# Loading the first pair of heads of the last pass in two halves, in a softmax-matmul kernel on one Trainium2 core

## The chip, the core and the metric

The kernel runs on one core of one Trainium2 chip. The core has five engines with instruction streams of their own: TensorE (PE, and PEld for its weight loads), VectorE (DVE), ScalarE (ACT), GpSimd (POOL) and SyncE (SP). They wait for each other through semaphores. Transfers between HBM and the on-chip memory are issued here by SyncE alone, all on one queue that 16 DMA engines serve.

The metric is the device time in microseconds of one execution. The times before the change are 1073.99, 1074.35 and 1074.74 us, so the median is 1074.35.

## The reference

For each of 8 x 12 = 96 heads, the scores are a 1024 x 1024 matrix and v is 1024 x 64, both float32:

```
scores_max = np.max(scores, axis=-1, keepdims=True)
attn = np.exp(scores - scores_max)
attn = attn / (np.sum(attn, axis=-1, keepdims=True) + 1e-8)
return np.matmul(attn, v).astype(np.float32)
```

The scores are 403 MB and have to be read once. The output and v are 25 MB each.

## The kernel before, in words

A pass of the loop over n0 (0, 4, ... 92: 24 passes) treats four heads as two pairs, k = 0 and k = 1. A pair is held as one tile of 128 partitions: 64 partitions per head, 16 score rows on each partition, 1024 scores per row. So one load of a pair is 128 x 16 x 1024 float32, 8.39 MB, and there are two such tiles, `s_nat0` for k = 0 and `s_nat1` for k = 1. In what follows a "row" r (0 to 15) is one row on each of the 128 partitions.

For a pair, `heads()` goes through the 16 rows:

- ScalarE takes the exponential of two rows at a time into `p_nat`, in float16 and without subtracting the maximum (line 368). For the second half of the second pair it takes one row at a time. There are eight `p_nat` buffers of two rows. Each pass loads ScalarE's function table once ahead of its first exponential.
- TensorE transposes each row in eight pieces into `psT` (line 381).
- VectorE copies two rows from PSUM to `pt` (line 393; line 389 for the rows taken one at a time).
- TensorE multiplies with `vones`, which holds v and columns of ones so that the sums of the exponentials come out too (`finish()`, line 152). It does so three rows behind the transposes (`LAG`).
- VectorE inverts the sums and normalises three rows at a time into `out_sb` (lines 132 and 140).

After the last row of k = 0, GpSimd spreads the next v into `vones` (`spread_v`, line 239) and SyncE stores the pair's output (`store`, line 170). At row 7 of k = 0 VectorE also scans `vones` (`watch_v`, lines 250 and 260). At the end of a pass `last()` spreads v for k = 1, loads the next second pair, stores the finished one and loads the next v. `judge()` (lines 276 to 292) then checks with VectorE and one tiny matmul on TensorE that the sums lie within bounds. If they ever didn't, `general()` would compute everything again behind the loop. TensorE's instructions have a fixed order, that of the program (`in_line`).

Transfers also have a fixed order among themselves (`queue`, line 120). Each transfer is made to follow the one queued before it by `after`; `apart` declares two instructions independent of each other. A load of a pair into its tile has to wait until the exponentials have read the rows that it overwrites, and the exponentials of a row wait for the transfer that brought it.

Two places already treat the ends of the run in another way. Ahead of the loop the very first pair is loaded in two halves of 8 rows. And in pass n0 = 88, the last but one, `last()` loads the second pair of the last pass in pieces of 4, 4, 3, 2, 1, 1 and 1 rows, with the store of pass 88's second pair between the third and the fourth piece. It chooses by a real branch (`tc.If`).

The first pair of the next pass is loaded in `heads()` after the last row of k = 0, by one transfer with a condition, so that the last pass skips it:

```
if r == R - 1 and k < K - 1:
    load(k, (n0 + (AHEAD + T * k)) % BH, cond=n0 < BH - AHEAD)
```

With `K` = 2 this is k = 0 alone. `AHEAD` is 4, `T` is 2, `R` is 16 and `BH` is 96. A transfer with a condition is an instruction that stands in every pass; where the condition is false no data moves, and its semaphore is still advanced for those who wait for it.

The loop has no barrier between passes (`iteration_sync="reg_based"`): each engine branches back by itself and goes on as its own waits allow.

Of the kernel before, what the change touches and what calls it, by code (L numbers as in the profile page):

```python
# [26 lines left out]
def kernel(  # L27
# [12 lines left out]
    BH = B * H  # L40
# [5 lines left out]
    AHEAD = 4  # L46
# [6 lines left out]
    T = 2  # L53
    K = AHEAD // T
    W = P // T
    R = SQ // W
# [39 lines left out]
    def take(bufs):  # L96
        k = turn.get(id(bufs), 0)
        turn[id(bufs)] = k + 1
        return bufs[k % len(bufs)]

    pending = []
    queued = []
# [11 lines left out]
    def in_line(op):  # L114

        if line:
            after(op, line[-1])
        line.append(op)

    def queue(dma):  # L120

        if queued:
            after(dma, queued[-1])
        queued.append(dma)
# [22 lines left out]
    def finish(u):  # L147

        n0, k, r, pt, st = u
        g, i = r // G, r % G  # L150
        for c in range(C):
            product = nc.tensor.matmul(  # L152
                out=st["psO"][g][:, i * M : (i + 1) * M],
                lhsT=pt[:, c * P : (c + 1) * P],
                rhs=vones[:, k, c].rearrange("p t n -> p (t n)")[:, 0:M],
                start=(c == 0),
                stop=(c == C - 1),
            )
            in_line(product)
        if i == G - 1 or r == R - 1:  # L160
            normalise(k, st, g)
        if r == R - 1 and k < K - 1:
            spread_v(k)
            store(n0, k)
# [30 lines left out]
    def apart(a, b, reason="stores of two heads are disjoint"):  # L195
        tc.declare_no_dep(a.ins, b.ins, across_iterations=True, reason=reason)

    def rewrite(buf, op):


        others = writers.setdefault(buf.name, [])
        for other in others:
            apart(op, other, "readers in between")
            apart(other, op, "readers in between")
        apart(op, op, "readers in between")
        others.append(op)

    def other_bank(tile, bank, op):

        for other in users.setdefault((tile.name, 1 - bank), []):  # L210
            apart(op, other, "banks are disjoint")
            apart(other, op, "banks are disjoint")
        users.setdefault((tile.name, bank), []).append(op)

    def load(k, n, parts=(R,), r=0, **cond):
        rows_n = sc_rows[bass.ds(n // T, 1)].rearrange("o x r k -> (o x) r k")
        for rows in parts:
            queue(
                nc.sync.dma_start(  # L219
                    out=s_bufs[k][:, r : r + rows, :], in_=rows_n[:, r : r + rows, :], **cond  # L220
                )
            )
            r += rows

    def load_v(n):

        rows = v_bh.rearrange("(m x) y -> m x y", x=P)
        queue(
            nc.sync.dma_start(
                out=v_sb[:].rearrange("x h s l d -> x (h s l d)"),  # L230
                in_=rows[bass.ds(n // AHEAD, 1)].rearrange("o x y -> (o x) y"),
            )
        )
# [14 lines left out]
    def watch_v(behind):  # L248

        watch = nc.vector.tensor_reduce(  # L250
            out=most,
            in_=vones[:, :, :, :, 0:D].rearrange("p k c t d -> p k (c t) d"),
            axis=mybir.AxisListType.XYZ,
            op=ALU.max,
            apply_absolute_value=True,
        )
        after(watch, behind)
        watches.append(watch)
        for bound, op in ((V_MIN, ALU.is_ge), (V_MAX, ALU.is_le)):
            nc.vector.scalar_tensor_tensor(  # L260
                out=fits, in0=most, scalar=bound, in1=fits, op0=op, op1=ALU.mult
            )
# [9 lines left out]
    def judge(bank):  # L272

        n = K * R
        part = small("part")
        nc.vector.tensor_reduce(out=seen[:, 0:1], in_=seen[:, 0 : n + 1], axis=X, op=ALU.min)  # L276
        nc.vector.tensor_reduce(  # L277
            out=seen[:, n + 1 : n + 2], in_=seen[:, 1 : n + 2], axis=X, op=ALU.max
        )
        nc.vector.scalar_tensor_tensor(  # L280
            out=part, in0=seen[:, n + 1 : n + 2], scalar=1.0, in1=fits, op0=ALU.is_le, op1=ALU.mult
        )
        nc.vector.scalar_tensor_tensor(  # L283
            out=right, in0=seen[:, 0:1], scalar=1.0 / SUM_MAX, in1=part, op0=ALU.is_ge, op1=ALU.mult
        )
        cell = bank[0:1, G * M : G * M + 1]
        in_line(
            nc.tensor.matmul(  # L288
                out=cell, lhsT=right[:], rhs=vones[:, 0, 0, 0, D : D + 1], start=True, stop=True
            )  # L290
        )
        nc.vector.tensor_copy(out=count[:], in_=cell)  # L292
# [45 lines left out]
    def last(n0):  # L338

        before = queued[-1:]  # L340
        k = K - 1
        with tc.If(n0 < BH - AHEAD) as cmp:
            spread_v(k)
            with tc.If(n0 < BH - 2 * AHEAD) as cmp2:
                queued[:] = before
                load(k, (n0 + (AHEAD + T * k)) % BH)
                store(n0, k)
                load_v((n0 + 2 * AHEAD) % BH)
            with cmp2.Else():
                queued[:] = before  # L350
                load(k, BH - T, (4, 4, 3))
                store(n0, k)
                load(k, BH - T, (2, 1, 1, 1), 11)
        with cmp.Else():
            queued[:] = before
            end()

    def heads(n0):

        for k in range(K):  # L360
            st = dict(psO=[take(psO_bufs) for g in range(GROUPS)])
            for r in range(R):
                late = k == K - 1 and r >= R // 2
                if r % EB == 0:
                    p_nat, psT2, pt2 = take(p_bufs), take(psT_bufs), take(pt_bufs)
                    rows = 1 if late else EB
                    for g in range(0, EB, rows):
                        exp = nc.scalar.activation(  # L368
                            out=p_nat[:, g : g + rows, :].rearrange(
                                "p r (x v) -> p x r v", v=Q * L  # L370
                            ),
                            in_=s_bufs[k][:, r + g : r + g + rows, :].rearrange(
                                "p r (i x l) -> p x (r i) l", i=Q, l=L
                            ),
                            func=EXP,
                        )
                        rewrite(p_nat, exp)
                p_row = p_nat[:, r % EB, :].rearrange("p (h q l) -> p h l q", q=P, l=L)
                psT, pt = psT2[:, r % EB, :], pt2[:, r % EB, :]
                for c in range(C):  # L380
                    turned = nc.tensor.transpose(  # L381
                        out=psT[:, c * P : (c + 1) * P],
                        in_=p_row[:, c // L, c % L, :],
                        identity=ident16[:],
                    )
                    in_line(turned)
                    other_bank(psT2, r % EB, turned)
                if late:
                    copy = nc.vector.tensor_copy(out=pt, in_=psT)  # L389
                    rewrite(pt2, copy)  # L390
                    other_bank(psT2, r % EB, copy)
                elif r % EB == EB - 1:
                    copy = nc.vector.tensor_copy(out=pt2[:], in_=psT2[:])  # L393
                    rewrite(pt2, copy)
                if k == 0 and r == R // 2 - 1:
                    watch_v(copy)
                if r == R - 1 and k < K - 1:
                    load(k, (n0 + (AHEAD + T * k)) % BH, cond=n0 < BH - AHEAD)
                pending.append((n0, k, r, pt, st))
                if len(pending) > LAG:  # L400
                    finish(pending.pop(0))
        while pending:
            finish(pending.pop(0))
        last(n0)
        judge(st["psO"][-1])

    assert BH % AHEAD == 0 and BH >= 2 * AHEAD and SK == Q * S * C and K == 2
    load_v(0)
    for k in range(K):
        load(k, T * k, (R // 2, R // 2) if k == 0 else (R,))  # L410
    for k in range(K):
        spread_v(k)
    load_v(AHEAD)
    with tc.For_i(
        0, BH, AHEAD, iteration_sync="reg_based"
    ) as n0:
        queued.clear()
        line.clear()
        heads(n0)
# [37 lines left out]
```

## Time and profile before

| What | Value |
|---|---|
| Median of 3 runs | 1074.35 us (1073.99 to 1074.74) |
| Profiled execution, its own time | 1074.52 us |
| Profiled execution, span from the first to the last instruction | 1072.8 us |
| Mean granted TensorE clock | 0.896 of full speed |
| TensorE matmuls busy | 793.8 us (74%) |
| VectorE busy | 768.7 us (72%) |
| ScalarE busy | 737.2 us (69%) |
| GpSimd busy | 239.2 us (22%) |
| Moved by transfers | 453.06 MB, mean 422 GB/s |

All times inside the run are counted from the start of the span. The last pass, n0 = 92, works on heads 92 to 95; its first exponential starts at 1029.48. The pass before it is n0 = 88, "pass 88", and its first exponential starts at 985.83. In rows of groups or of the timeline, "x8" is a count of instructions, and a bracket at the end holds the engine's idle time before them and what ended it. "L219" is line 219 of the kernel; all loads of scores have that line, since it is the line of the helper `load`.

### The profile page before, as it was taken

Reading aid. Unit: us, or ns where it says so; the run is one execution under the profiler, and the core shown is the slowest. Engines: PE = TensorE matmul, PEld = TensorE weight load, DVE = VectorE, ACT = ScalarE, POOL = GpSimd, SP = SyncE. Lnnn points to the kernel's source line nnn. Section 1 sums busy time; section 2 is a strip of 40 time slices with the busy share of each in tenths; the row PEclk is TensorE's granted clock in tenths of the full one; section 3 lists DMA queues with packets and bytes.
Section 4 is the critical chain, followed back from the end, with each engine's and each line's share of the span. In section 5 each row is a group of like instructions: output and inputs, shape, how many; then the busy total and the mean of one; then the engine's idle time right before and its main releaser. Section 6 shows DMA issues by size and latency. Waiting matters only on the chain.

```text
span 1072.8 us, 32527 instructions
## 1 busy us (share of the span) xinstructions
PE 793.8 (74%) x12312; PEld 757.8 (71%) x12312; DVE 768.7 (72%) x1539; ACT 737.2 (69%) x504; POOL 239.2 (22%) x399
## 2 busy tenths in 40 slices
PE   2578678776786777866877678677786697867867
PEld 2578578676686776866877668677686686866867
DVE  1569668685686776966778568687696686866868
ACT  3567668667686586766866768658676686676864
POOL 3031131121311212113122131130211311113111
PEclk9889889898898988989989889898898898988989
DMA  9999999999999999999999999999999999999991
GB/s 408 448 409 411 440 440 447 413 427 453 415 445 421 456 413 447 413 432 445 447 415 426 452 413 447 423 457 411 450 411 429 451 442 418 427 452 411 450 409 70
DMA packets 18436, 453.06 MB, mean 422 GB/s; under 512 B 2048, under 2 KB 2176, under 8 KB 8704
## 3 DMA queue, kind: packets, MB, share of 16 engines
q1 hardware_dynamic: 18432, 452.99, 98.1%
q8 instruction: 4, 0.07, 0.0%
HBM read 436.21 MB, written 25.17 MB: 430 GB/s over the span
## 4 chain that ended last, share of the span: by engine, by line
DMA 60%; ACT 27%; issue 7%; PE 2%; DVE 1%; PEld 1%; ACTq 1%; SPq 0%; DVEq 0%
DMA s_nat<-in_scores_dram 60%; ACT p_nat L368 27%; PE psT L381 1%; PE psO L152 1%; ACTq L368 1%; DVE pt L393 1%; PEld L381 0%; PEld L152 0%; DVE most L250 0%; ACT L368 0%; SPq L219 0%; DVE pt L389 0%; DVE out_sb L140 0%; DVE seen L132 0%; DVE seen L276 0%
## 5 line engine op out<-in xcount | busy, mean ns | idle before, releaser
L368 ACT ACTIVATE p_nat<-s_nat 128x2048 f16<-128x2048 f32 (+1 forms) x480 | 706.4, 1557 | 118.1 <-PE psO L152 38.0
L381 PE MATMUL psT<-ident,p_nat 128*128 128x128 f16 x6144 | 506.0, 233 | 171.0 <-ACT p_nat L368 171.0
L381 PEld LDWEIGHTS <-p_nat 128*128 128x128 f16 x6144 | 425.6, 119 | 181.0 <-ACT p_nat L368 181.0
L393 DVE COPY pt<-psT 128x2048 f16<-128x2048 f16 x288 | 352.4, 1224 | 266.7 <-PE L381 170.0
L152 PE MATMUL psO<-vones,pt 128*128 128x130 f16 x6144 | 486.2, 223 | 63.0 <-DVE fits L260 40.4
L152 PEld LDWEIGHTS <-pt 128*128 128x128 f16 x6144 | 387.3, 99 | 84.8 <-DVE pt L393 55.8
L239 POOL CAST vones<-v_sb 32x512 f16<-32x512 f32 x392 | 238.5, 608 | 818.5 <-PE psT L381 418.1
L140 DVE TENSOR_TENSOR out_sb<-psO,seen 64x192 f32<-64x192 f32 (+1 forms) x576 | 191.8, 333 | 18.0
L368 ACT ACT_TABLE_LOAD x24 | 30.8, 1283 | 203.5 <-DMA s_nat<-in_scores_dram 186.8
L389 DVE COPY pt<-psT 128x1024 f16<-128x1024 f16 x192 | 123.5, 685 | 2.3
L250 DVE TENSOR_REDUCE most<-vones 128x1 f32<-128x2048 f16 x24 | 54.9, 2286 | 0.8
L132 DVE RECIPROCAL seen<-psO 128x3 f32<-128x3 f32 (+1 forms) x288 | 49.3, 171 | 2.8 <-PE L381 0.8
L288 PE MATMUL psO<-vones,right 128*1 128x1 f16 x24 | 3.9, 164 | 41.0 <-DVE right L283 41.0
L288 PEld LDWEIGHTS <-right 128*1 128x1 f16 x24 | 1.9, 79 | 45.3 <-DVE right L283 45.3
L292 DVE CAST count<-psO 1x1 int32<-1x1 f32 x24 | 3.5, 147 | 6.2 <-PE psO L288 6.2
L260 DVE SCALAR_TENSOR_TENSOR fits<-most,fits 128x1 f32<-128x1 f32 x48 | 7.4, 155 | 0.0
L280 DVE SCALAR_TENSOR_TENSOR part<-seen,fits 128x1 f32<-128x1 f32 x24 | 5.3, 222 | 0.8
L276 DVE TENSOR_REDUCE seen<-seen 128x1 f32<-128x33 f32 x24 | 4.5, 188 | 0.8
L283 DVE SCALAR_TENSOR_TENSOR right<-seen,part 128x1 f16<-128x1 f32 x24 | 3.9, 163 | 0.8
L277 DVE TENSOR_REDUCE seen<-seen 128x1 f32<-128x33 f32 x24 | 4.2, 176 | 0.0
L77 DVE MEMSET vones<- 128x64 f16 x1 | 0.1, 112 | 0.8 <-PEq L441 0.8
L74 DVE CAST ident<-ident 128x128 f16<-128x128 f32 x1 | 0.2, 227 | 0.4 <-POOL ident masks.py:199 0.4
(8 smaller groups left out, 1.1 us busy)
## 6 DMA issues: line engine op xcount, KB each, us to landing
v_sb<-in_v_dram SPq DMA_DIRECT2D x24, 1024.0 KB, 22.2
out_dram<-out_sb SPq DMA_DIRECT2D x47, 512.0 KB, 16.7
s_nat<-in_scores_dram SPq DMA_DIRECT2D x2, 4096.0 KB, 18.6
s_nat<-in_scores_dram SPq DMA_DIRECT2D x2, 2048.0 KB, 22.5
s_nat<-in_scores_dram SPq DMA_DIRECT2D x1, 1536.0 KB, 27.4
s_nat<-in_scores_dram SPq DMA_DIRECT2D x3, 512.0 KB, 21.0
s_nat<-in_scores_dram SPq DMA_DIRECT2D x1, 1024.0 KB, 20.6
s_nat<-in_scores_dram SPq DMA_DIRECT2D x47, 28.4
```

The lines of the kernel that those rows point to most:

```text
L132: nc.vector.reciprocal(out=recip, in_=psO[:, :, D : D + 1])
L140: nc.vector.tensor_tensor(out=out_bufs[k][part, g * G : g * G + rows, :], in0=psO[part, :, t * N : t * N + D], in1=recip[part].to_broadcas ...
L152: product = nc.tensor.matmul(out=st["psO"][g][:, i * M : (i + 1) * M], lhsT=pt[:, c * P : (c + 1) * P], rhs=vones[:, k, c].rearrange("p t ...
L239: spread = nc.gpsimd.tensor_copy(out=vones[s * Q : (s + 1) * Q, k, :, t, 0:D].rearrange("i (h l) d -> i h l d", l=L), in_=v_sb[(k * T + t) ...
L250: watch = nc.vector.tensor_reduce(out=most, in_=vones[:, :, :, :, 0:D].rearrange("p k c t d -> p k (c t) d"), axis=mybir.AxisListType.XYZ, ...
L260: nc.vector.scalar_tensor_tensor(out=fits, in0=most, scalar=bound, in1=fits, op0=op, op1=ALU.mult)
L280: nc.vector.scalar_tensor_tensor(out=part, in0=seen[:, n + 1 : n + 2], scalar=1.0, in1=fits, op0=ALU.is_le, op1=ALU.mult)
L288: nc.tensor.matmul(out=cell, lhsT=right[:], rhs=vones[:, 0, 0, 0, D : D + 1], start=True, stop=True)
L368: exp = nc.scalar.activation(out=p_nat[:, g : g + rows, :].rearrange("p r (x v) -> p x r v", v=Q * L), in_=s_bufs[k][:, r + g : r + g + ro ...
L381: turned = nc.tensor.transpose(out=psT[:, c * P : (c + 1) * P], in_=p_row[:, c // L, c % L, :], identity=ident16[:],)
L389: copy = nc.vector.tensor_copy(out=pt, in_=psT)
L393: copy = nc.vector.tensor_copy(out=pt2[:], in_=psT2[:])
```

## The change

The load in `heads()` becomes a call of a new function, `load_first`, which issues three transfers where there was one:

```
+    def load_first(n0):
+
+        at = len(queued)
+        load(0, (n0 + AHEAD) % BH, cond=n0 < BH - 2 * AHEAD)
+        load(0, BH - AHEAD, (R // 2, R // 2), cond=(n0 == BH - 2 * AHEAD))
+        for half in queued[at + 1 :]:
+            apart(half, queued[at], "one of both is skipped, and readers are in between")
+            apart(queued[at], half, "one of both is skipped, and readers are in between")
...
                 if r == R - 1 and k < K - 1:
-                    load(k, (n0 + (AHEAD + T * k)) % BH, cond=n0 < BH - AHEAD)
+                    load_first(n0)
```

The first transfer is the old one, now under the condition n0 < 88: it brings the first pair of the next pass whole, in all passes but the last two. The other two bring rows 0 to 7 and rows 8 to 15 of heads 92 and 93, and their condition is n0 = 88. So passes 0 to 84 move the whole pair and skip both halves, pass 88 skips the whole transfer and moves both halves, and the last pass skips all three. The whole transfer and the halves write the same tile; `apart` declares them independent of each other.

In the compiled kernel SyncE's order is: first half, whole, second half. The first half waits for the exponentials of pass n0 that read rows 0 to 7, the whole transfer for all eight exponentials of the pair; the second half stands behind that wait. The first exponential of a pass waits for the first half and for the whole transfer, and that of rows 8 and 9 for the second half too. All other engines have the same instructions in the same order as before. The later transfers use other semaphores of the eight that transfers take turns on.

## The prediction

> **What bounds the kernel now.** I read the page first, for which resource is full over the whole run. Columns of the third part: packets, MB, share of the span that the 16 DMA engines spent on them.
>
> ```profile
> span 1072.8 us, 32527 instructions
> ...
> q1 hardware_dynamic: 18432, 452.99, 98.1%
> q8 instruction: 4, 0.07, 0.0%
> HBM read 436.21 MB, written 25.17 MB: 430 GB/s over the span
> ## 4 chain that ended last, share of the span: by engine, by line
> DMA 60%; ACT 27%; issue 7%; PE 2%; DVE 1%; PEld 1%; ACTq 1%; SPq 0%; DVEq 0%
> ```
>
> The one queue that carries every transfer is busy for 98.1% of the span. Over the passes it is the bound, and nothing on an engine shortens it. What can be gained lies after the last load has landed. So I went to the stretches at the end, with their busy time per engine, the granted clock, the share of the DMA engines and GB/s:
>
> ```profile
> 1024.00:1028.00 4.00, 0.65 (x9) 0.38 (x7) 2.06 (x10) 0.00 (x0) 3.05 (x5) 0.84 0.77 324
> 1028.00:1034.00 6.00, 2.56 (x24) 2.39 (x25) 0.62 (x1) 5.80 (x4) 1.83 (x3) 0.50 1.02 437
> 1034.00:1040.00 6.00, 6.00 (x84) 6.00 (x83) 3.81 (x6) 6.00 (x4) 0.00 (x0) 0.75 0.95 408
> 1040.00:1046.00 6.00, 4.31 (x76) 4.15 (x74) 5.88 (x10) 6.00 (x5) 0.00 (x0) 1.00 1.02 425
> 1046.00:1050.00 4.00, 3.87 (x67) 3.57 (x64) 3.80 (x9) 4.00 (x3) 0.00 (x0) 1.00 0.48 197
> 1050.00:1056.00 6.00, 5.87 (x104) 5.71 (x102) 5.65 (x10) 6.00 (x7) 2.65 (x5) 1.00 0.00 0
> ```
>
> The loads are over by about 1050, yet the program runs on to 1072.8: over 22 us in which TensorE and VectorE work off the last pass. From 1040 VectorE (third busy figure) is full: 5.88 of 6 us, then 3.80 of 4 and 5.65 of 6. And from 1024 to 1034 TensorE (first figure) does 3.2 us of work in 10. That gap is where the change aims. ScalarE shows why:
>
> ```profile
> 985.83 14.53 ACT L368 ACTIVATE p_nat<-s_nat 128x2048 f16<-128x2048 f32 x8
> 1005.11 14.91 ACT L368 ACTIVATE p_nat<-s_nat 128x2048 f16<-128x2048 f32 x12 [4.76 <-PE psT L381]
> 1028.18 1.28 ACT L368 ACT_TABLE_LOAD   x1 [8.17 <-DMA s_nat<-in_scores_dram]
> 1029.48 29.32 ACT L368 ACTIVATE p_nat<-s_nat 128x2048 f16<-128x2048 f32 x20
> ```
>
> It finishes pass 88 at 1020.02 and then sits 8.17 us until the 8 MB load of heads 92 and 93 has landed whole. The chain and SyncE's issues place that load:
>
> ```profile
> 1000.58 27.52 DMA s_nat<-in_scores_dram
> ```
>
> ```profile
> 1000.58 0.34 SPq L219 DMA_DIRECT2D s_nat<-in_scores_dram  x1
> 1012.69 0.36 SPq L170 DMA_DIRECT2D out_dram<-out_sb  x1
> 1013.84 1.78 SPq L219 DMA_DIRECT2D s_nat<-in_scores_dram  x3
> ```
>
> Issued at 1000.58, landed at 1028.10. Its 8.39 MB take 19.5 us at 430 GB/s, so its own transfer begins near 1008.6; before that the queue works on older transfers.
>
> **Step 1: when the first half lands.** In the compiled order of SyncE the first half now stands ahead of the skipped whole load and waits only for the exponentials of rows 0 to 7 of pass 88, four of the eight in the row of 14.53 us, so it can be issued near 985.83 + 7.3 = 993.1 instead of 1000.58. The queue is still busy with older transfers then, so it lands earlier only by the half that is behind it: 4.19 MB at 430 GB/s are 9.8 us, hence 1018.3. The second half keeps 1028.10. This needs the queue to deliver in order of issue. The start of the program shows that it does, where two halves and a whole load are issued within 1.7 us:
>
> ```profile
> 1.19 1.70 SPq L219 DMA_DIRECT2D s_nat<-in_scores_dram  x3
> ```
>
> ```profile
> 16.72 1.28 ACT L368 ACT_TABLE_LOAD   x1 [16.72 <-SPq L414]
> 18.01 14.54 ACT L368 ACTIVATE p_nat<-s_nat 128x2048 f16<-128x2048 f32 x8
> 45.74 14.90 ACT L368 ACTIVATE p_nat<-s_nat 128x2048 f16<-128x2048 f32 x12 [13.19 <-DMA s_nat<-in_scores_dram]
> ```
>
> ScalarE starts on the first half by 16.72 and the whole load behind it frees the next group only at 45.74. Shared service would have brought them together.
>
> **Step 2: ScalarE.** Free at 1020.02, data there since 1018.3. With the table load (1.28) and up to 1 us of loop branch, its first exponential of 1.82 us (14.53 / 8) is done by about 1024.2 instead of 1031.3. All 20 need 29.32 us, so they end near 1051.7, against 1058.80; the last load lands by 1050. Between the last exponential and the end of the span lay 14.0 us, and with the end that comes out below there are 15.7, so ScalarE doesn't become the bound.
>
> **Step 3: TensorE starts when pass 88 lets it.** It is in order, and judge() of pass 88 ends at 1026.35. Its loop branch follows:
>
> ```profile
> 1026.19 0.16 PE L288 MATMUL psO<-vones,right 128*1 128x1 f16 x1 [1.71 <-DVE right L283]
> 1031.44 1.90 PE L381 MATMUL psT<-ident,p_nat 128*128 128x128 f16 x16 [5.09 <-ACT p_nat L368]
> ```
>
> ```profile
> L414 PEldq COMPARE_BRANCH  x1: 228/228/228, 1026.7 to 1026.7; - x1
> ```
>
> So the restart moves from 1031.44 to about 1027.1: 4.3 us. The 10 us of the half load shrink to this, because pass 88 occupies TensorE and VectorE until then.
>
> **Step 4: the clock after the restart.** The granted clock of 0.84 over 1024 to 1028 and of 0.75 over 1034 to 1040 put the half-speed stretch at 1026.7 to 1037.0: 5.6 us of it came after the restart, when work was there. How long will it last after the earlier restart? An earlier pass start tells:
>
> ```profile
> 132.00:135.85 3.85, 1.65 (x26) 1.32 (x25) 2.60 (x5) 2.49 (x2) 0.00 (x0) 1.00 1.10 470
> 135.85:139.27 3.42, 3.42 (x36) 3.42 (x33) 1.51 (x3) 3.42 (x3) 0.00 (x0) 0.50 1.45 628
> ```
>
> There half speed began while TensorE was busy throughout, and lasted 3.42 us. With a restart right at the beginning of the half-speed stretch I take the same, until 1030.1. Now the steps at the restart, by VectorE's rows:
>
> ```profile
> 1033.38 1.23 DVE L393 COPY pt<-psT 128x2048 f16<-128x2048 f16 x1 [6.84 <-PE L381]
> 1035.18 1.23 DVE L393 COPY pt<-psT 128x2048 f16<-128x2048 f16 x1 [0.57 <-PE L152]
> 1037.96 1.23 DVE L393 COPY pt<-psT 128x2048 f16<-128x2048 f16 x1 [1.55 <-PE psO L152]
> 1039.10 0.17 DVE L132 RECIPROCAL seen<-psO 128x3 f32<-128x3 f32 x1
> 1039.30 0.74 DVE L140 TENSOR_TENSOR out_sb<-psO,seen 64x192 f32<-64x192 f32 x2
> ```
>
> Two rows' transposes cost 1.90 us at half speed, so the first copy starts at 1029.0 and the second at about 1030.5. Before the third come four groups of eight matmuls at full speed, each as in the chain:
>
> ```profile
> 1052.34 0.46 PE psO L152 x8
> ```
>
> That is 1.8 us: third copy at 1032.4, not 1037.96. It is 5.5 us earlier, 4.3 from the restart and 1.2 from the shorter half-speed stretch. From there VectorE is full and its work is the same, so the end moves by the same. If half speed lasted 5.6 us again, until 1032.7, four of the groups would run slow and the gain would be 4.0; if the clock stayed whole, 6.5. I take 5.5, the row nearest in kind (a start without idle time). TensorE's speed after the restart cannot gain more than half of 5.6, so 4.3 + 2.8 = 7.1 is the upper end.
>
> By the Trainium skill (TensorE: Matmul & The Clock Gate, "What's actually happening"), the gate works on free-running windows of about 3.4 us and opens after one busy window. By that rule the stretch would be cut at the first window boundary behind a busy window, wherever that falls in this run, and the gain would be anything from 4.0 to 6.5. The 3.42 us above agree.
>
> **Step 5: what else waits.** The first write to out_sb of the last pass, 1039.30, moves to 1033.8. It must follow the store issued at 1012.69, which is behind the second half in the queue: 0.52 MB after 1028.10 end at 1029.3, so there are 4 us left. The vones of the second pair are spread by 1030 (the 1.83 us of GpSimd from 1028), needed later. The transfers of the second pair keep their times.
>
> **Step 6: all other passes.** Each issues two skipped transfers more on SyncE. The one skip in the trace is the last pass's:
>
> ```profile
> L219 SPq DMA_DIRECT2D s_nat<-in_scores_dram x1: 113/113/113, 1049.1 to 1049.1; - x1
> ```
>
> Its 113 ns is the lower bound; the upper is that of a real issue with its waits, 1.78 / 3 = 0.59 us. The first skip falls into SyncE's wait for ScalarE; the second comes behind the real load and ahead of a store issued 12 us later. At worst some tenths delay the load's issue, and the queue has 8 us of older work then. I take 0; uncovered, 2 x 0.113 to 2 x 0.59 us over 23 passes are 5.2 to 27 us. ScalarE's added waits (well under 0.1 us a pass) have the same cover.
>
> **The sum.** Against the profiled execution's own 1074.52 (span 1072.8 and 1.7 around it): 1074.52 - 5.5 = 1069.0. The median of the runs shown, 1074.35, lies 0.17 lower, so 1068.9.
>
> **Rivals.**
> 1. *TensorE doesn't restart that early*, since the first instructions of the body aren't at hand after the branch. The 4.5 us between 1026.95 and 1031.44 would hide that now. At the full 4.5 only the second and later copies gain, for the exponentials are ready and the queue of work is deep: about 2 us, so 1072.4; half of it gives 1070.6. Against it: 4 instruction packets on q8 in the whole run, for 24 passes.
>    The Trainium skill (Runtime: NRT & Kernel Launch, "Instruction fetch mechanics") says that a taken branch out of the prefetched pages stalls for a fetch. The same page's sizes would let this loop body stay resident; no run here shows which holds.
> 2. *The half isn't early*: its condition or its waits bind it to the whole load's landing, or the halves are served together. Then ScalarE starts at 1028 as now: 1074.35. The start of the program speaks against it.
> 3. *Slower: the skips lengthen every pass.* If the semaphore of a skipped transfer comes late or the skip holds up the queue, each of 23 passes pays. From 0.24 us a pass the gain of 5.5 is gone, from 0.33 it measures as slower; at 0.59 for each of the two, 1074.35 + 27 - 5.5 = 1096. Only a drained queue could show this, and at 98.1% it isn't drained.
>
> **How the numbers follow.** What a measurement here can tell from no change is about 0.2%, 2.15 us. The forecast (gain 4.0 to 7.1, times 1067.2 to 1070.4) has 0.77. Rival 1 has 0.09, of which 0.03 ends within 0.2%. Rival 2 has 0.06, rival 3 has 0.08. So faster 0.83, same 0.09, slower 0.08. The range runs from the upper bound of the gain, 1067.2, into rival 1, 1071.8, and leaves out about 0.17.
>
> **What would show it.** Right: in the profile after, ScalarE's last idle time before the table load shrinks from 8.17 to under 1.5 us, two issues of 4096 KB stand in pass 88 near 993 and 1001, TensorE restarts at 1027 to 1028, the third copy stands near 1032.4, and all passes before 88 keep their times within 1 us. Wrong: a restart at 1029 or later with exponentials ready (rival 1), a table load still at 1028 (rival 2), or a pass 88 that starts over 1 us later than 985.8 (rival 3).

## The result, and the profile after

The changed kernel takes 1069.49 us (median; 1069.34 to 1070.31), beside 1074.19 us (1073.79 to 1074.74) for the kernel before. The ratio is 0.9958, with a 95% interval of 0.9945 to 0.9970: faster by 4.7 us. The profiled execution took 1069.46 us with a span of 1067.5 us, 5.3 us less than the span before.

The page of the changed kernel, the same lines as before:

```profile
span 1067.5 us, 32791 instructions
...
q1 hardware_dynamic: 18576, 452.99, 98.6%
q8 instruction: 4, 0.07, 0.0%
HBM read 637.53 MB, written 25.17 MB: 621 GB/s over the span
```

The queue moved the same 452.99 MB and is still busy nearly all the time. It has 144 packets more, which is one transfer: 18,432 packets for the 128 transfers before and 18,576 for 129 now are 144 each. Pass 88 now issues two transfers for one. The 48 skipped transfers (46 halves and 2 wholes) left no packet. The last line shown is a trap: "HBM read" grew by 201.3 MB, which is 46 skipped halves of 4.19 MB and one skipped whole load of 8.39 MB more than before. That figure counts skipped transfers as if they had run; the packets and MB of the queue say what ran.

SyncE's issues of scores in pass 88, the first half at 993.30, the skipped whole load and the second half behind it:

```profile
993.30 7.98 SPq L219 DMA_DIRECT2D s_nat<-in_scores_dram  x3
```

The end of the run in stretches (TensorE, its weight loads, VectorE, ScalarE, GpSimd, then the granted clock, the share of the DMA engines and GB/s):

```profile
1024.00:1028.00 4.00, 1.39 (x20) 1.16 (x19) 2.06 (x10) 4.00 (x3) 3.05 (x5) 0.96 1.04 440
1028.00:1034.00 6.00, 6.00 (x83) 6.00 (x81) 3.68 (x4) 6.00 (x5) 1.83 (x3) 0.74 1.03 441
1034.00:1040.00 6.00, 4.32 (x76) 4.11 (x74) 5.87 (x10) 6.00 (x5) 0.00 (x0) 1.00 0.95 406
1040.00:1046.00 6.00, 5.80 (x96) 5.34 (x94) 5.74 (x11) 5.91 (x5) 0.00 (x0) 1.00 1.02 424
1046.00:1050.00 4.00, 3.94 (x70) 3.94 (x71) 3.76 (x9) 3.24 (x4) 1.90 (x4) 1.00 0.49 202
1050.00:1056.00 6.00, 5.99 (x106) 5.83 (x104) 5.69 (x11) 1.62 (x2) 2.96 (x5) 1.00 0.21 87
```

VectorE is now full from 1034, not from 1040. TensorE does 7.4 us of work between 1024 and 1034 instead of 3.2. The loads still end near 1050, as before. ScalarE, TensorE and VectorE around the start of the last pass, each from the timeline of its engine:

```profile
985.86 14.53 ACT L377 ACTIVATE p_nat<-s_nat 128x2048 f16<-128x2048 f32 x8
1005.11 14.90 ACT L377 ACTIVATE p_nat<-s_nat 128x2048 f16<-128x2048 f32 x12 [4.73 <-PE L390]
1020.04 1.28 ACT L377 ACT_TABLE_LOAD   x1
1021.33 24.57 ACT L377 ACTIVATE p_nat<-s_nat 128x2048 f16<-128x2048 f32 x15
1046.76 4.86 ACT L377 ACTIVATE p_nat<-s_nat 128x1024 f16<-128x1024 f32 x5 [0.85 <-PE L390]
```

```profile
1026.20 0.16 PE L297 MATMUL psO<-vones,right 128*1 128x1 f16 x1 [1.71 <-DVE right L292]
1027.26 3.23 PE L390 MATMUL psT<-ident,p_nat 128*128 128x128 f16 x32 [0.90 <-ACT p_nat L377]
```

```profile
1028.82 1.22 DVE L402 COPY pt<-psT 128x2048 f16<-128x2048 f16 x1 [2.27 <-PE L390]
1030.52 1.23 DVE L402 COPY pt<-psT 128x2048 f16<-128x2048 f16 x1 [0.48 <-PE L152]
1032.77 1.23 DVE L402 COPY pt<-psT 128x2048 f16<-128x2048 f16 x1 [1.02 <-PE psO L152]
1033.91 0.17 DVE L132 RECIPROCAL seen<-psO 128x3 f32<-128x3 f32 x1
1034.11 0.74 DVE L140 TENSOR_TENSOR out_sb<-psO,seen 64x192 f32<-64x192 f32 x2
```

ScalarE's 8.17 us of idle time are gone: it goes from the last exponential of pass 88 straight to the table load. TensorE restarts at 1027.26 instead of 1031.44, 4.18 us earlier. The 0.90 us before that are put down to ScalarE, but the first exponential had ended at about 1023.2. In them TensorE's sequencer goes through the end of the pass, with two branches of 0.23 us each at 1026.3 and 1026.7. VectorE's third copy stands at 1032.77 instead of 1037.96, 5.19 us earlier, and the end of the span follows it by the same 34.7 to 34.8 us in both kernels.

### The profile page after: what moved, and what is told of

Read it like the earlier page. It is cut to its first block, busy times and chain, and to the rows that moved or that the text cites. A ratio compares the mean times of both kernels' runs of the same rounds, so it can differ in the third digit from the quotient of the medians.

```text
span 1067.5 us, 32791 instructions
## 1 busy us (share of the span) xinstructions
PE 793.6 (74%) x12312; PEld 757.7 (71%) x12312; DVE 768.8 (72%) x1539; ACT 737.3 (69%) x504; POOL 239.2 (22%) x399
## 3 DMA queue, kind: packets, MB, share of 16 engines
q1 hardware_dynamic: 18576, 452.99, 98.6%
HBM read 637.53 MB, written 25.17 MB: 621 GB/s over the span
## 4 chain that ended last, share of the span: by engine, by line
DMA 58%; ACT 27%; issue 6%; PE 3%; PEld 2%; DVE 2%; ACTq 1%; SPq 0%; PEldq 0%; DVEq 0%
DMA s_nat<-in_scores_dram 58%; ACT p_nat L377 26%; PE psO L152 1%; PEld L390 1%; PE psT L390 1%; DVE pt L402 1%; PEld L152 1%; ACTq L377 1%; DVE most L259 0%; ACT L377 0%; DVE pt L398 0%; SPq L219 0%; ACTq L423 0%; DVE seen L132 0%; DVE out_sb L140 0%
```

## The experiments

The theory to test has four parts: the skipped transfers cost nothing; what counts is that the rows which are needed first land earlier, in order of issue; the end of pass 88 on TensorE, not the data, then sets the restart; and about 1 us of what is left is TensorE at half speed behind the restart. The edits below are against the changed kernel; parts that are left out are marked with dots.

**Two skips more, and nothing else.** The whole load runs in every pass as before; the halves never do.

```diff
-        load(0, (n0 + AHEAD) % BH, cond=n0 < BH - 2 * AHEAD)
-        load(0, BH - AHEAD, (R // 2, R // 2), cond=(n0 == BH - 2 * AHEAD))
+        load(0, (n0 + AHEAD) % BH, cond=n0 < BH - AHEAD)
+        load(0, BH - AHEAD, (R // 2, R // 2), cond=(n0 == BH))
```

> The kernel before with two skipped half loads more in every pass (a condition that is never true) and the whole load left as it was. My theory (the skips lie under SyncE's own waits and under the 8 us of older work in the queue): no change, 1074.2 within 0.5 us, and the load of the last pass's first pair is issued within 0.3 us of 1000.6 and lands at 1028.1. Rival (each pass pays for its skips, 0.11 to 0.59 us each): 5 to 27 us longer over 23 passes, 1079 to 1101.

Measured: 1073.94 us (1073.55 to 1074.90) against 1074.26, ratio 0.9996 (0.9986 to 1.0005). ScalarE's row for the last pass:

```profile
1028.12 1.28 ACT L377 ACT_TABLE_LOAD   x1 [8.12 <-DMA s_nat<-in_scores_dram]
```

The load lands at 1028.1 as before, after 23 passes with two more skips each. Rival 3 of the prediction is out: its smallest price was 5.2 us, and the interval ends at 0.5 us.

**The halves in the other order.** Rows 8 to 15 are transferred first.

```diff
-        load(0, BH - AHEAD, (R // 2, R // 2), cond=(n0 == BH - 2 * AHEAD))
+        load(0, BH - AHEAD, (R // 2,), R // 2, cond=(n0 == BH - 2 * AHEAD))
+        load(0, BH - AHEAD, (R // 2,), 0, cond=(n0 == BH - 2 * AHEAD))
```

> The changed kernel with its two halves in the other order: rows 8 to 15 are transferred first and rows 0 to 7 behind them. Transfers, bytes, conditions and skips are the same. My theory (the gain is that the rows which are needed first arrive 10 us earlier): the first exponential of the last pass waits until about 1028 again, TensorE restarts near 1031.4, 1074.2 within 0.7 us. Rival (the gain comes from something else that the change brings, smaller transfers or other semaphores): 1069.5.

Measured: 1074.38 us (1073.46 to 1074.91), ratio 0.9998 (0.9989 to 1.0008).

```profile
1028.37 1.28 ACT L378 ACT_TABLE_LOAD   x1 [8.14 <-DMA s_nat<-in_scores_dram]
```

Same transfers, same bytes, and no gain: ScalarE sits 8.14 us again. So neither the split in itself nor the other semaphores bring anything; the early landing of rows 0 to 7 does. One thing is not separated: in this kernel the first half is also issued at 1000.83, since rows 8 to 15 are free later.

**Pieces of 14 and 2 rows.**

```diff
-        load(0, BH - AHEAD, (R // 2, R // 2), cond=(n0 == BH - 2 * AHEAD))
+        load(0, BH - AHEAD, (14, 2), cond=(n0 == BH - 2 * AHEAD))
```

> The changed kernel with pieces of 14 and 2 rows instead of 8 and 8. My theory (the queue delivers in order of issue at 430 GB/s, and a restart of TensorE before 1027.3 is not to be had): the first piece lands at 1008.6 + 14/16 of 19.5 = 1025.7, the first exponential ends near 1028.9, TensorE restarts then, 1.6 us later than with halves, and some more goes to a longer half-speed stretch: 1070.7 to 1072.2, I take 1071.3. Rival 1 (the size of the first piece doesn't matter as long as there are two): 1069.5. Rival 2 (the pieces are served together and land together at 1028): 1074.2.

Measured: 1071.63 us (1070.94 to 1072.17), ratio 0.9974 (0.9963 to 0.9985). ScalarE, then TensorE:

```profile
1025.90 1.28 ACT L377 ACT_TABLE_LOAD   x1 [5.75 <-DMA s_nat<-in_scores_dram]
```

```profile
1029.16 3.70 PE L390 MATMUL psT<-ident,p_nat 128*128 128x128 f16 x32 [2.68 <-ACT p_nat L377]
```

Here the landing of the first piece can be read, since ScalarE waits for it: just under 1025.90, where 1025.7 was worked out from 430 GB/s and order of issue. Pieces that were served together would have landed at 1028. TensorE restarts 1.9 us later than with halves, now truly held by an exponential, and the time is 2.1 us longer.

**Pieces of 4 and 12 rows**, the same edit with (4, 12).

> The changed kernel with pieces of 4 and 12 rows. My theory: the first piece lands near 1013.5, before ScalarE is free at 1020.0, so it gains nothing over 8 rows; ScalarE takes rows 0 to 3 until 1025 and then waits for the second piece at 1028.1; TensorE restarts at 1027.3 as with halves but gets rows 4 and 5 only at 1030.1 and rows 6 and 7 at 1031.9, about when it comes to them: 1069.5, up to 0.7 us later. Rival (an earlier first landing always helps): below 1069.

Measured: 1070.52 us (1069.41 to 1070.89), ratio 0.9964 (0.9951 to 0.9977). ScalarE:

```profile
1021.66 3.71 ACT L377 ACTIVATE p_nat<-s_nat 128x2048 f16<-128x2048 f32 x2
1028.49 25.73 ACT L377 ACTIVATE p_nat<-s_nat 128x2048 f16<-128x2048 f32 x18 [3.11 <-PE L390]
```

A smaller first piece gains nothing: data ahead of 1020 meets an engine that isn't free. It then costs ScalarE 3.11 us in the middle. The row puts these down to TensorE, but 1028.49 is about when the second piece lands (1028.1 in the kernel before, and pass 88 starts 0.38 us later in this execution). TensorE restarted at 1027.54 and was busy throughout from 1028 to 1034, so it didn't run out of exponentials:

```profile
1024.00:1028.00 4.00, 1.26 (x14) 1.03 (x15) 2.35 (x12) 1.38 (x1) 2.77 (x5) 0.75 0.78 329
1028.00:1034.00 6.00, 6.00 (x69) 6.00 (x67) 2.58 (x3) 5.51 (x4) 2.14 (x4) 0.60 1.01 434
```

The clock of 0.75 and 0.60 makes 6.8 us at half speed, from 1026.0 to 1032.8, twice the length in the changed kernel. Whether the median's 1 us against the halves is more than that isn't settled: the times of both overlap.

**judge() in the last pass alone.** Minimum and maximum are still gathered in each pass; the matmul, the two operations ahead of it and the copy behind it move into the branch of `last()` that ends the run. There the matmul is no longer part of TensorE's fixed order (`in_line`).

```diff
-        last(n0)
-        judge(st["psO"][-1])
+        gather()
+        last(n0, st["psO"][-1])
...
             end()
+            judge(bank)
```

> The changed kernel with the tiny matmul of judge() and the three VectorE instructions around it moved into the branch that only the last pass takes; the minimum and maximum are still gathered in every pass, so the same is computed. TensorE then doesn't wait for VectorE at the end of pass 88. My theory (with halves, the end of pass 88 on TensorE sets the restart): restart near 1025.3 instead of 1027.3, and a shorter half-speed stretch or none, 2.0 to 3.3 us less than with the change alone: 1066.2 to 1067.5. Rival (the restart is held by the branch and the instructions behind it, or by the exponentials): 1069.5 within 0.5 us.

Measured: 1067.30 us (1066.44 to 1068.06), ratio 0.9932 (0.9916 to 0.9949). TensorE:

```profile
1023.91 0.63 PE L152 MATMUL psO<-vones,pt 128*128 128x130 f16 x8 [0.74 <-DVE pt L401]
1025.61 1.95 PE L393 MATMUL psT<-ident,p_nat 128*128 128x128 f16 x32 [1.06 <-DVE out_sb L140]
```

The restart moves to 1025.61, with 32 transposes in 1.95 us instead of 3.23: no half speed is left there. That answers the prediction's rival 1, too. TensorE goes through the branch and into the body at full pace 1.06 us after its last product, so nothing at the branch had held it at 1027.3; the matmul of judge() had.

**The same with the whole load.**

> The kernel before with judge() in the last pass's branch alone and the one whole load. My theory (without the halves the last pass waits for the load, whatever TensorE does before): first exponential and restart stay at 1029.5 and 1031.4, 1074.2 within 0.5 us. So the 2 us of the run with both come from the halves and the shorter pass end together. Rival (the shorter pass end is worth 2 us by itself): 1072.1.

Measured: 1074.17 us (1073.43 to 1074.99), ratio 1.0000 (0.9990 to 1.0009).

```profile
1031.45 2.85 PE L384 MATMUL psT<-ident,p_nat 128*128 128x128 f16 x24 [6.95 <-ACT p_nat L371]
```

The shorter pass end is worth nothing alone: TensorE just waits 6.95 us instead of 5.09. It pays only once the data is early.

**Filling TensorE's gap, in a bank that VectorE still reads.** 28 matmuls of 120 columns into unused columns of the last `psO` buffer, ahead of judge().

```diff
...
+        warm(st["psO"][-1])
         last(n0)
         judge(st["psO"][-1])
```

> The changed kernel with 28 matmuls of 120 columns, whose results nobody reads, between the last products of a pass and judge(), where TensorE waits 1.7 us for VectorE. The rest is the same. My theory (1.0 to 1.3 us of the last pass is TensorE at half speed after the restart, and half speed comes from the idle time ahead of it): the granted clock stays at or near 1.00 from 1024 to 1034, the restart stays near 1027.3, the third copy comes near 1031.6 instead of 1032.8, and the time is 1 us less than with the change alone, 1068.5. Rival (half speed costs nothing, since VectorE sets the pace): 1069.5; and the filling itself, 28 x 0.06 = 1.7 us, must not push judge() back, or 1070 and more.

Measured: 1072.90 us (1072.11 to 1074.11), ratio 0.9990 (0.9981 to 0.9999), 3.4 us longer than the change alone. A miss: the time doesn't show what the run was made for. TensorE, and then the waits of SyncE from 1062 on:

```profile
1026.10 1.63 PE L308 MATMUL psO<-ident 128*128 128x120 f16 x28 [0.94 <-DVE out_sb L141]
1027.66 0.16 PE L298 MATMUL psO<-vones,right 128*1 128x1 f16 x1
1027.90 1.95 PE L400 MATMUL psT<-ident,p_nat 128*128 128x128 f16 x32
```

```profile
SPq L472 <- PEq L472: 4.5, 3, 3.3
```

The filling waits for VectorE to normalise out of the same buffer and so pushes judge() back, in the last pass too. The larger part, 2.7 of the 3.5 us by which the span is longer, comes behind VectorE's last instruction. It is the wait in the second fence (total, times, longest): the closing barrier waits 3.3 us for TensorE's sequencer. In the kernel before, as in the changed one, the longest such wait was 0.4:

```profile
SPq L452 <- PEq L452: 1.0, 3, 0.4
```

The rows of the last pass do show the half speed gone: the clock is 1.00 over 1024 to 1034, and the third copy starts at 1032.55, 4.65 us after the restart at 1027.90, instead of 5.51.

**The same filling, another bank and few instructions.** Seven matmuls of 512 columns into `psO_bufs[0]`; beside it on the same chip ran the change alone and the kernel with judge() in the last pass.

```diff
...
+        fill()
         last(n0)
         judge(st["psO"][-1])
```

> The changed kernel with 7 matmuls of 512 columns between the last products of a pass and judge(). They write a bank of PSUM that VectorE has done with, so that they start at 1024.5 without a wait and end, at 0.22 us each, near 1026.0, before judge() at 1026.2. Nobody reads their results. My theory (1.0 to 1.3 us of the last pass is half speed after the restart): the granted clock stays 1.00 from 1024 to 1034, the restart stays near 1027.3, the third copy of the last pass comes near 1031.5, and the time is about 1 us less than that of the change alone in the same job. Rival (VectorE sets the pace there anyway): the same time as the change alone.

> The changed kernel itself beside the other two, for the comparison on one chip: 1069.5 within 0.7 us. My theory takes the spread between its executions (1069.3 to 1070.3) for the half-speed stretch, which begins and ends at other places in each execution.

> The changed kernel with judge() in the last pass's branch alone, again, for an interval of its own: 2 to 3 us less than the change alone, 1066.5 to 1067.5.

Measured: 1068.56 us with the filling (1068.38 to 1069.21; ratio 0.9951, 0.9937 to 0.9965), 1069.79 for the change alone (1069.52 to 1070.46; 0.9963, 0.9949 to 0.9977), 1066.78 with judge() once (1066.61 to 1067.09; 0.9932, 0.9918 to 0.9946). Of the filled kernel TensorE, the stretches and VectorE:

```profile
1024.27 1.67 PE L307 MATMUL psO<-vones,ident 128*128 128x512 f16 x7
1026.15 0.16 PE L297 MATMUL psO<-vones,right 128*1 128x1 f16 x1 [0.20 <-DVE right L292]
1027.16 1.95 PE L403 MATMUL psT<-ident,p_nat 128*128 128x128 f16 x32 [0.85 <-ACT p_nat L390]
```

```profile
1024.00:1028.00 4.00, 2.95 (x32) 1.81 (x29) 2.01 (x10) 4.00 (x3) 3.09 (x6) 1.00 0.94 396
1028.00:1034.00 6.00, 5.42 (x96) 5.29 (x95) 4.46 (x7) 6.00 (x5) 1.82 (x3) 1.00 1.03 440
```

```profile
1028.32 2.35 DVE L415 COPY pt<-psT 128x2048 f16<-128x2048 f16 x2 [1.82 <-PE L403]
1031.80 1.23 DVE L415 COPY pt<-psT 128x2048 f16<-128x2048 f16 x1 [1.13 <-PE psO L152]
```

TensorE and VectorE of the changed kernel that ran beside it:

```profile
1027.61 3.18 PE L390 MATMUL psT<-ident,p_nat 128*128 128x128 f16 x32 [0.85 <-ACT p_nat L377]
```

```profile
1033.00 1.22 DVE L402 COPY pt<-psT 128x2048 f16<-128x2048 f16 x1 [0.92 <-PE psO L152]
```

The clock stays whole, the restart follows judge()'s matmul by 1.01 us in both, and the third copy comes 4.64 us after it instead of 5.39 here and 5.51 in the first profile of the change. So 0.8 to 0.9 us of the changed kernel's last pass was half speed. Useless work in an idle gap made the kernel 1.2 us faster by the medians. Of these, 0.8 to 0.9 are seen in the rows; the rest is within the 0.4 us by which the start of the last pass differs between executions (restart at 1027.26 and at 1027.61 for the same kernel).

The version to keep is that with judge() in the last pass: it beats both kernels, by 7.3 us and by 3.0 us, and computes the same.

## Why the prediction was right, point by point

The forecast was 1068.9 us and the kernel takes 1069.49. The mechanism was right; the size came out close in part by luck, as steps 2 and 4 show.

- *Step 1, landing.* The first half was issued at 993.30 (forecast 993.1). Its landing can't be read, since nobody waited for it; the run with 14 rows confirms the rate and the order to 0.2 us for a first piece of that size.
- *Step 2, ScalarE.* No time for the loop branch was needed: the table load follows at 1020.04. The last exponential ended at 1051.62, as forecast (1051.7), but only because two errors cancelled: ScalarE started about 1 us earlier than forecast and then waited 0.85 us for TensorE at 1046. It is not the bound, as forecast.
- *Step 3, the restart.* Forecast 1027.1, measured 1027.26. That pass 88 and not the data sets it was shown from both sides: with data there only at 1025.9 (14 and 2 rows) it moves, with data earlier than needed (4 and 12) it doesn't, and without judge() in pass 88 it goes to 1025.61.
- *Step 4, the clock.* This is the term with the error. The stretch was taken as 3.4 us from 1026.7, ending at 1030.1. The clock of 0.96 over 1024 to 1028 and 0.74 over 1028 to 1034 make it 3.4 us, from 1027.7 to 1031.1. The length was right and the place was not (in the second profile of the change, with 0.85 and 0.81, the stretch lies at 1026.8 to 1030.3), and so the step gave 1.0 us, not 1.2, and the third copy came at 1032.77, not 1032.4. This agrees with the Trainium skill (TensorE: Matmul & The Clock Gate, "What's actually happening"), whose windows of 3.4 us run free of the kernel. That the length was right was partly luck. Worked out in the same way from the clock, half speed lasted 3.4 and 3.5 us in the two profiles of the change, 6.8 us with 14 and 2 rows (clock 0.89 and 0.51 over the same stretches) and with 4 and 12, and 10.3 us in the kernel before: one, two or three times 3.4 us. With 4 and 12 TensorE restarted 0.07 us earlier than in the second profile of the change, but the stretch had begun 0.8 us earlier. It was busy for 2.0 of the first 3.4 us there and got a second 3.4 us at half speed; in that profile of the change it was busy for 2.6 and half speed ended. Also, at whole clock the third copy comes 4.64 us after the restart, so the rows would have gained 6.1 us at most, not the 6.5 that the step allows, nor the 7.1 of its upper end.
- *Step 5, the store.* The first write to out_sb moved to 1034.11 (forecast 1033.8) with no wait ahead of it.
- *Step 6, the skips.* Zero, as taken: pass 88 starts at 985.86 beside 985.83, and two skips alone changed nothing.
- *The sum.* In the profiled executions the end moved by 5.3 us, where 5.5 was forecast. Between the medians it is 4.7. The profiled execution before, 1074.52, was 0.33 above its median, and other executions of the change, up to 1070.31, are longer than the profiled one. Those left no trace. A second 3.4 us at half speed, which brought the third copy 0.9 us later with 4 and 12 rows, would account for such a spread; that is argued, not shown.

## What to carry to other kernels

This kernel is bound by its transfers, and its last load lands near 1050 before and after the change; what got shorter is the work that is left over behind that landing. So look in the last pass for an engine that waits for a whole load when it needs its first rows. The gain is not the time by which the rows come earlier (10 us here, by the prediction's estimate) but what the next engine lets through (its restart moved 4.2 us, and 1.0 came from the clock). Then it is worth shortening that engine's end, which was worth nothing before (judge() in the last pass alone takes 1074.17 us beside 1074.19 with the whole load, and 1066.78 beside 1069.79 with the halves). Two skipped transfers more in each pass cost nothing that shows here, on a queue that is busy for 98% of the span; no run here has a queue that drains.

## What the runs showed that I had not expected

- 56 instructions more on TensorE (28 matmuls and their weight loads) went with 3.3 us at the very end of the program, just behind TensorE's branch over `general()` to the closing barrier: the branch starts at 1066.8, and but for one instruction of 0.07 us TensorE's sequencer does nothing more until 1070.6. With 14 more there was no such wait (1068.56 us). The Trainium skill (Runtime: NRT & Kernel Launch, "Instruction fetch mechanics") says that a taken branch to a page of instructions that isn't at hand has to fetch it first. That would fit a body whose length moves the branch's target into another page, but no run isolated it, and the changed kernel, too, has one packet on the instruction queue (q8) at its end, near 1066.5, without such a wait: the place and the size are measured, the cause is argued.
- Idle time cost twice here. The 1.7 us that TensorE waited for VectorE ahead of judge() cost 0.8 to 0.9 us more afterwards, through the clock, and 1.67 us of useless matmuls in that gap took this back.
- A page's "HBM read" can count transfers that were skipped: 637.53 MB, where the scores and v are 402.65 + 25.17 = 427.8 MB. The 436.21 MB of the kernel before hold one such transfer already, the 8.39 MB that the last pass skips.
